# A two-layer hybrid trunk on one core: joint feed-forward weights loaded after the first down product, gate matmuls written later, the second mixer at half pace, and q, k, v loaded a chunk ahead

## The chip, the cores and the metric

The kernel runs on one core of one Trainium2 chip. The metric is the device time in microseconds of one execution. TensorE (PE in the profile) does the matmuls and the 128x128 transposes, VectorE (DVE) and ScalarE (ACT) the elementwise work, GpSimd (POOL) a few subtractions and powers, and SyncE (SP) issues every load and store.

## The reference

The input is x of 1024 rows and 1024 columns in float32. Two layers follow, each with a mixer and a SwiGLU feed-forward between RMS norms:

```python
h = _rmsnorm(x, pre_mix_g[layer])
h = mixer(h)                                   # layer 0: conformer conv + RG-LRU; layer 1: mLSTM
x = x + _rmsnorm(h, post_mix_g[layer])
h = _swiglu(_rmsnorm(x, pre_ffn_g[layer]), ...)  # (silu(x Wg) * (x Wu)) Wd, 2816 hidden columns
x = x + _rmsnorm(h, post_ffn_g[layer])
```

The mixer of layer 0 multiplies the normed rows with one input projection of 2048 columns. One half goes through a gated causal convolution of 31 taps, a LayerNorm and a swish (the conformer). The other half goes through a convolution of 4 taps, two sigmoid gates from a block-diagonal matmul, a linear recurrence and a product with a GeLU branch (the LRU). The concatenated results go through an output projection. The mixer of layer 1 is an mLSTM: q, k, v, an output gate and two gate rows per head come from one projection, and a matrix memory of 8 heads is carried along the rows in chunks.

## The kernel before, in words

All wide products are done as three matmuls of float32 halves: each operand is split into a rounded part (hi, a cast on ACT) and a remainder (lo, a subtraction on DVE or POOL), and `mm3` (L124 to L128) adds hi·hi, hi·lo and lo·hi in PSUM. The 1024 rows are worked in two halves of 512 rows, A and B, so that the mixer or norm of one half stands beside the matmuls of the other.

**Written order and order on the engines.** The main line of matmuls is a set of Python generators. `run` (L1165) steps one of them, and each of its steps has a cost. `step` (L1145) adds cost times pace to every side generator that was handed to `start` (L1140), and advances it once per whole unit. So the pace says how densely a side's instructions are written between the main line's. When the program is built, a scheduler takes, for each engine, the earliest written instruction whose inputs and buffers are ready by its own reckoning. The written order is thus a priority and not the order in which an engine runs. On the chip each engine, and SP as well, works through its list in order and waits at its head.

**Buffers.** The pools set how far work can run ahead: 5 `raw` weight tiles of 512 KB (`raw_tile`, L87), 4 `hi` and 4 `lo` tiles (L90), 30 `unit` and 13 `small` tiles (L51), 4 PSUM banks for the main line and 4 (`ps_aux`) for everything else.

**Layer 0.** `in0` (L711) computes the 16 blocks of the input projection. `mixer0` (L863) alternates between `lrus` (L848) and `conformer` (L803). The conformer's 31 taps are 30 operations on DVE per tile (`pcv`, L754), four tiles to a half. `lru` (L767) runs the 4-tap convolution into `xr` and then, for each of two gates, takes a PSUM tile `pg`, yields once, and writes the matmul (L775), which reads `xr`. Mixer A runs at pace 1.2 beside `in0` of both halves. After 12 of the 16 blocks of half B come the output projection of half A (`Project`, `popA`/`pooA` tiles) with `sandwich` (L202, post-norm, residual, pre-norm and the transposes `ptnoA`) as a side, the last 4 blocks of half B with their GeLU (`gel`, L729), and then `phase0` of the feed-forward for 10 of its 11 blocks. Mixer B starts before the last chunk of that projection, at the pace `PACE_B` of 1.2. It has to be done before the output projection of half B (`pooB`), which follows `phase0(EARLY)`.

**Feed-forward.** Both halves together go through a Strassen-like scheme with 11 blocks of hidden columns. `phase0` computes the products of half A. `down_first` (L594) is the first of the down products: for each of 11 blocks `prep2` (L558) loads one raw tile `r20a` (layer 1: `r21a`), splits it into `whid0a` and `wlod0a`, and 12 matmuls add into the tiles `d`. Beside it `feature_b` transposes half B (`ptnoB`, `ptnpB`) and makes the sums and differences of the two halves (`xs`, `xb`, `xa`, `xk`) with DVE. `phase1` needs these and the joint weights: `prep1a` (L432) loads four raw tiles for a block (`ri`, `rj` of gate and up) and two products of phase 0 (`u2`), forms eight differences on POOL (`t14`, `t23`) and splits `rj`; `prep1b` (L460) splits the differences. `f.begun = f.prep1a(0)` is written before `down_first`, in both layers.

**Layer 1.** `in1` writes v (24 steps), then 8 blocks of q and k, then 8 blocks of the output gate o (`pimo`). For half B the first 32 steps stand beside `mlstm` of half A, which then is drained; the 8 blocks of o follow the output projection of half A (`popA`), beside `sandwich`. `mlstm` (L949) works in 4 chunks of 128 rows per half: at the head of a chunk SP loads the broadcast decay rows `ab` (written a moment before to `da`) and `iwb`, then `qk` and `vt`; PE transposes k (`pk`, L1011), multiplies q and k (`sc`), the scores with v (`pn`), updates the state (`pu`), and transposes the result (`ph`, L1090) after a norm on ACT, POOL and DVE.

Of the kernel before, what the change touches and what calls it, by code (L numbers as in the profile page):

```python
# [14 lines left out]
P = 128  # L15
# [25 lines left out]
def trunk(ctx: ExitStack, tc: tile.TileContext, x, w_in, w_out, w_gate, w_up, w_down,  # L41
# [12 lines left out]
    def unit(shape, dt=F32, name="u"):  # L54
        return up.tile(shape, dt, tag="u", name=name, bufs=NU)
# [269 lines left out]
    class Ffn:  # L325
# [146 lines left out]
        def phase1(self, ms):  # L472
            l = self.l
            ms = list(ms)
            w_next = self.prep1b(ms[0], *self.begun)
            for _ in self.rest:
                pass
            for n, m in enumerate(ms):
                w, h11 = w_next
                u2 = [w[k]["u2"] for k in range(2)]  # L480
                u3, c21, b, c = [], [], [], []
                for k in range(2):
                    a = ps_main(f"pa{l}{m}{k}")
                    self.product(a, w[k]["t2"], self.ops["s2"], True)
                    TT(u2[k], a, u2[k], op=OP.add)
                    yield 2.8
                for k in range(2):
                    b.append(ps_main(f"pb{l}{m}{k}"))
                    self.product(b[k], w[k]["t3"], self.ops["s3"], True)
                    u3.append(small([P, T], f"u3{l}{m}{k}"))  # L490
                    TT(u3[k], b[k], u2[k], op=OP.add)
                    yield 2.8
                if n + 1 < len(ms):
                    w_next = self.prep1(ms[n + 1])
                for k in range(2):
                    c.append(ps_aux([P, T], f"pc{l}{m}{k}"))
                    self.product(c[k], w[k]["t1"], self.ops["s1"], True)
                    TT(u3[k], c[k], u3[k], op=OP.add)
                    yield 2.8
                nc.scalar.activation(u3[0], u3[0], AF.Silu)  # L500
                for k in range(2):
                    self.product(b[k], w[k]["t4"], self.ops["a22"], False)
                    c21.append(small([P, T], f"c21{l}{m}{k}"))
                    TT(c21[k], b[k], u2[k], op=OP.add)
                    yield 2.8
                TT(u3[0], u3[0], u3[1], op=OP.mult)
                nc.sync.dma_start(self.d_s["a22"][m], u3[0])
                nc.scalar.activation(c21[0], c21[0], AF.Silu)
                for k in range(2):
                    self.product(c[k], w[k]["b22"], self.ops["s4"], False)  # L510
                    TT(u2[k], c[k], u2[k], op=OP.add)
                    yield 2.8
                nc.scalar.activation(u2[0], u2[0], AF.Silu)
                TT(c21[0], c21[0], c21[1], op=OP.mult)
                TT(u2[0], u2[0], u2[1], op=OP.mult)
                self.sums(m, h11, u2[0], c21[0], u3[0])
# [250 lines left out]
    def lru(m, j, res):  # L767
# [4 lines left out]
        for i in range(2):  # L772
            ps = ps_aux([P, T], f"pg{h}{j}{i}")
            yield
            nc.tensor.matmul(ps, lw[:, i * 4 + j], xr, start=True, stop=True)  # L775
            s = small([P, T], f"sg{h}{j}{i}")
            nc.scalar.activation(s, ps, AF.Sigmoid, bias=V(("b_a", "b_x")[i], j))
            g.append(s)
# [170 lines left out]
    def mlstm(m):  # L949
# [39 lines left out]
        nc.sync.dma_start(d_w[h], iw)  # L989
        yield  # L990
        m.yT = []
        for c in range(NT):
            cs = slice(c * P, (c + 1) * P)
            ab = unit([P, 8, P], F32, f"ab{h}{c}")
# [2 lines left out]
            dw = d_w[h].rearrange("(a s) j -> s a j", s=2)  # L997
            for s in range(2):
                nc.sync.dma_start(iwb[s * 64:(s + 1) * 64], dw[s, :, cs].partition_broadcast(64))
            qk = unit([P, 8, P], F32, f"qk{h}{c}")  # L1000
            nc.sync.dma_start(qk, d_qk[h][:, :, cs].rearrange("a p j -> p a j"))
            vt = unit([P, 8, 129], F32, f"vt{h}{c}")
            nc.sync.dma_start(vt, d_v[h][c])
            pc = ps_aux([P, 40], f"pc{h}{c}")
            nc.tensor.transpose(pc, ce[:, cs], ident[0:40, 0:40])
            cem = sp.tile([P, 40], F32, tag="cem", name=f"cem{h}{c}", bufs=2)
# [49 lines left out]
            if not (h == 1 and c == NT - 1):  # L1056
                for i in range(4):
# [3 lines left out]
                    for s in range(2):  # L1061
# [2 lines left out]
                                                       iwb[rr, i, P - 1:P], pu[rr, s],  # L1064
                                                       op0=OP.mult, op1=OP.add)
                    yield
            ss = sp.tile([P, 8], F32, tag="hss", name=f"hss{h}{c}", bufs=2)
            for hd in range(8):
                junk = sp.tile([P, P], BF16, tag="junkh", name=f"jh{h}{c}{hd}", bufs=1)
# [53 lines left out]
    W.pool = len(W.src)  # L1123
    src_in1()
    src_in1()
    o_part = W.src[-8:]
    del W.src[-8:]
    src_proj(m_out, OUT1)
    W.src += o_part
    src_ffn(1, EARLY)  # L1130
# [9 lines left out]
    def start(gen, pace):  # L1140
        s = [gen, pace, 0.0]
        sides.append(s)
        return s
# [50 lines left out]
    run(gb, CUT)  # L1194
    until(sa, lambda: all(4 + j in ma.yT for j in range(4)))
    oa = Out("oA")
    ga = start(sandwich(oa, x, x1, post_mix[0:1], 0, gf(0), f0.feature_a), 1.2)
    sb = []

    def second_mixer():  # L1200
        drain(sa)
        sb.append(start(mixer0(mb), PACE_B))

    run(Project(ma.yT, oa, OUT0).run(second_mixer))
    sb = sb[0]
    run(gb)
    drain(ga)
    run(f0.phase0(EARLY))
    drain(sb)
    ob = Out("oB")  # L1210
    gb = start(sandwich(ob, x, x1, post_mix[0:1], 1, gf(0), f0.feature_b, 6), 1.0)
    run(Project(mb.yT, ob, OUT0).run())
    run(f0.phase0(LATE))
    f0.begun = f0.prep1a(0)
    run(f0.down_first())
    drain(gb)
    run(f0.phase1(range(HP)))
# [9 lines left out]
    gb = in1(nb, xmb)  # L1227
    run(gb, 32)
    drain(sa)
    pa = Out("pA")  # L1230
    ga = start(sandwich(pa, x2, x3, post_mix[1:2], 0, gf(1), f1.feature_a), 1.2)
    run(Project(na.yT, pa, OUT1).run())
# [6 lines left out]
    gb = start(sandwich(pb, x2, x3, post_mix[1:2], 1, gf(1), f1.feature_b, 6), 1.0)  # L1239
    run(Project(nb.yT, pb, OUT1).run())  # L1240
    run(f1.phase0(LATE))
    f1.begun = f1.prep1a(0)
    run(f1.down_first())
    drain(gb)
    run(f1.phase1(range(HP)))
# [95 lines left out]
```

## Time and profile before

| | us |
|---|---|
| median of 3 runs | 2179.38 (2175.66 to 2179.52) |
| the profiled execution | 2178.53 |
| its span, first to last instruction | 2176.7 |
| PE busy | 2071.7 (95%) |
| DVE busy | 1476.4 (68%) |
| ACT busy | 919.6 (42%) |
| POOL busy | 680.2 (31%) |

The profiled execution is 1.8 us longer than its span. A PE instruction's end is modelled and neighbours overlap, so busy time on PE is time in which it had something in hand, at whichever clock was granted: the granted clock of a stretch is given as a share of full speed, 1.00 for 2.4 GHz and 0.50 for 1.2 GHz.

### The profile page before, as it was taken

Reading aid. Unit: us, or ns where it says so; the run is one execution under the profiler, and the core shown is the slowest. Engines: PE = TensorE matmul, PEld = TensorE weight load, DVE = VectorE, ACT = ScalarE, POOL = GpSimd, SP = SyncE. Lnnn points to the kernel's source line nnn. Section 1 sums busy time; section 2 is a strip of 40 time slices with the busy share of each in tenths; the row PEclk is TensorE's granted clock in tenths of the full one; section 3 lists DMA queues with packets and bytes.
Section 4 is the critical chain, followed back from the end, with each engine's and each line's share of the span. In section 5 each row is a group of like instructions: output and inputs, shape, how many; then the busy total and the mean of one; then the engine's idle time right before and its main releaser. Section 6 shows DMA issues by size and latency. Waiting matters only on the chain.

```text
span 2176.7 us, 26097 instructions
## 1 busy us (share of the span) xinstructions
PE 2071.7 (95%) x9200; PEld 1680.8 (77%) x9200; DVE 1476.4 (68%) x2037; ACT 919.6 (42%) x1304; POOL 680.2 (31%) x453
## 2 busy tenths in 40 slices
PE   7989979997999999999999998999998999999998
PEld 6767756775888887787988987778876788888786
DVE  7999859347666677558653754546458977766567
ACT  5665575545222222446253333545445222223453
POOL 4344533443533436501010000300024544436311
PEclk9999989997999999999999999999999999999999
DMA  6232434555444459967473752657456544469966
GB/s 229 74 126 89 135 142 163 169 179 185 168 160 165 165 174 319 395 206 250 133 251 104 224 191 84 233 184 220 147 187 213 188 150 162 159 218 350 335 220 225
DMA packets 202739, 417.38 MB, mean 192 GB/s; under 512 B 19920, under 2 KB 48720, under 8 KB 202608
## 3 DMA queue, kind: packets, MB, share of 16 engines
q1 hardware_dynamic: 202608, 415.72, 56.0%
q8 instruction: 72, 1.18, 0.2%
q14 instruction: 59, 0.48, 0.1%
HBM read 302.82 MB, written 112.82 MB: 191 GB/s over the span
## 4 chain that ended last, share of the span: by engine, by line
PE 72%; DVE 13%; DMA 6%; issue 5%; ACT 3%; POOL 1%; SPq 0%; DVEq 0%; POOLq 0%; ACTq 0%
PE d L127 5%; PE d L128 5%; PE d L126 5%; DVE pcv L754 4%; PE pb L127 4%; PE pb L126 3%; PE pb L128 3%; PE pc L128 3%; PE pc L127 3%; PE pc L126 3%; PE p L126 3%; PE p L127 3%; PE p L128 3%; PE pa L128 2%; PE pa L126 2%
## 5 line engine op out<-in xcount | busy, mean ns | idle before, releaser
L107 ACT CAST whi<-raw 128x1024 fp32r<-128x1024 f32 (+2 forms) x164 | 164.3, 1005 | 234.1 <-PE pimo L127 49.9
L109 POOL TENSOR_TENSOR wlo<-raw,whi 128x1024 fp32r<-128x1024 f32 x66 | 166.6, 2530 | 230.6 <-ACT whi L107 192.4
L109 DVE TENSOR_TENSOR wlo<-raw,whi 128x1024 fp32r<-128x1024 f32 (+2 forms) x98 | 112.0, 1146 | 132.8 <-ACT whi L107 127.1
L754 DVE SCALAR_TENSOR_TENSOR pcv<-cy,vec,pcv 128x512 f32<-128x512 f32 x240 | 166.7, 746 | 0.6
L1078 POOL TENSOR_TENSOR hrr<-hss,half 128x8 f32<-128x8 f32 x8 | 13.1, 1641 | 251.5 <-DVE hss L1076 251.5
L132 DVE TENSOR_TENSOR wlod1s<-r21s,whid1s 128x1024 fp32r<-128x1024 f32 x44 | 55.2, 1260 | 49.1 <-ACT whid1s L131 48.6
L132 DVE TENSOR_TENSOR wlod0s<-r20s,whid0s 128x1024 fp32r<-128x1024 f32 x44 | 59.9, 1362 | 41.1 <-ACT whid0s L131 37.9
L126 PE MATMUL p<-xTnoA,whi 128*128 128x512 f32 x176 | 71.5, 411 | 7.7 <-ACT gel L729 5.9
L131 ACT CAST whid1s<-r21s 128x1024 fp32r<-128x1024 f32 x44 | 46.3, 1053 | 65.9 <-PE d L128 50.9
L131 ACT CAST whid0s<-r20s 128x1024 fp32r<-128x1024 f32 x44 | 46.3, 1053 | 61.1 <-PE d L128 54.1
L128 PE MATMUL p<-xTnoA,wlo 128*128 128x512 f32 x176 | 72.1, 413 | 0.0
L127 PE MATMUL p<-xTnoA,whi 128*128 128x512 f32 x176 | 71.5, 406 | 0.0
L127 PE MATMUL d<-wlod0s,whid0s 128*128 128x512 f32 x176 | 69.5, 395 | 2.1 <-DVE wlod0s L132 2.0
L126 PE MATMUL p<-xTnpA,whi 128*128 128x512 f32 x176 | 70.8, 405 | 0.0
L128 PE MATMUL p<-xTnpA,wlo 128*128 128x512 f32 x176 | 70.6, 401 | 0.0
L127 PE MATMUL p<-xTnpA,whi 128*128 128x512 f32 x176 | 70.2, 399 | 0.0
L127 PE MATMUL d<-wlod1s,whid1s 128*128 128x512 f32 x176 | 69.7, 396 | 0.0
L128 PE MATMUL d<-whid1s,wlod1s 128*128 128x512 f32 x176 | 69.5, 395 | 0.0
L128 PE MATMUL d<-whid0s,wlod0s 128*128 128x512 f32 x176 | 68.7, 390 | 0.0
L132 DVE TENSOR_TENSOR wlod0a<-r20a,whid0a 128x1024 fp32r<-128x1024 f32 x33 | 44.3, 1348 | 34.7 <-ACT whid0a L131 33.2
L126 PE MATMUL d<-whid1s 128*128 128x512 f32 x176 | 63.7, 397 | 3.2 <-ACT yeA L624 3.2
L548 POOL TENSOR_TENSOR wt<-wq 128x512 f32<-128x512 f32 x22 | 35.4, 1610 | 89.6 <-DMA wq<-in_w_down 44.0
(2483 smaller groups left out, 6660.7 us busy)
## 6 DMA issues: line engine op xcount, KB each, us to landing
wq<-in_w_down SPq DMA_DIRECT2D x88, 256.0 KB, 5.1
ft<-wt SPq DMA_DIRECT2D x88, 256.0 KB, 5.1
raw<-in_w_in SPq DMA_DIRECT2D x32, 512.0 KB, 3.5
raw<-in_m_in SPq DMA_DIRECT2D x32, 512.0 KB, 4.5
raw<-in_w_gate SPq DMA_DIRECT2D x22, 512.0 KB, 4.3
raw<-in_w_up SPq DMA_DIRECT2D x22, 512.0 KB, 3.8
fp<-p1f SPq DMA_DIRECT2D x44, 256.0 KB, 2.5
fs<-s SPq DMA_DIRECT2D x44, 256.0 KB, 2.3
```

Source lines behind the costliest of these rows:

```text
L107: nc.scalar.copy(hi[:, 0:n], raw[:, 0:n])
L109: eng.tensor_tensor(lo[:, 0:n], raw[:, 0:n], hi[:, 0:n].bitcast(F32), op=OP.subtract)
L126: nc.tensor.matmul(ps, l[0], r[0], start=first, stop=False, **kw)
L127: nc.tensor.matmul(ps, l[0], r[1], start=False, stop=False, **kw)
L128: nc.tensor.matmul(ps, l[1], r[0], start=False, stop=last, **kw)
L131: nc.scalar.copy(dst_hi, src)
L132: nc.vector.tensor_tensor(dst_lo, src, dst_hi.bitcast(F32), op=OP.subtract)
L548: sub(t[0][:, 0], q[0][:, 1], q[0][:, 0], op=OP.subtract)
L754: nc.vector.scalar_tensor_tensor(dst, src[:, k:k + T], V(wname, w0 + k), dst, op0=OP.mult, op1=OP.add)
L1078: nc.gpsimd.tensor_tensor(rr, ss, half, op=OP.pow)
```

## The change

Six edits. (1) In both layers `prep1a(0)` no longer stands before `down_first`; `phase1` calls the whole `prep1` for its first block, after `down_first` and after the side with `feature_b` is drained. (2) In `lru`, the first of the two gate matmuls is written four yields later. (3) Mixer B starts at pace 0.5 and goes to 1.2 when `phase0(EARLY)` begins. (4) `sandwich` of half A in layer 0 waits four steps before its transposes. (5) In `mlstm`, `qk` and `vt` of a chunk are loaded one chunk earlier: those of the first chunk before its `ab`, those of the next after the state update of this one. (6) In layer 1 two of the eight blocks of o of half B are written after `mlstm` of half A is drained, ahead of the output projection of half A; the list of weights is reordered to match.

```diff
         def phase1(self, ms):
             l = self.l
             ms = list(ms)
-            w_next = self.prep1b(ms[0], *self.begun)
+            w_next = self.prep1(ms[0])
...
             ps = ps_aux([P, T], f"pg{h}{j}{i}")
             yield
+            if i == 0:
+                for _ in range(4):
+                    yield
             nc.tensor.matmul(ps, lw[:, i * 4 + j], xr, start=True, stop=True)
...
+        def load(c):
+            qk = unit([P, 8, P], F32, f"qk{h}{c}")
+            nc.sync.dma_start(qk, d_qk[h][:, :, c * P:(c + 1) * P].rearrange("a p j -> p a j"))
+            vt = unit([P, 8, 129], F32, f"vt{h}{c}")
+            nc.sync.dma_start(vt, d_v[h][c])
+            return qk, vt
+
+        loaded = load(0)
         for c in range(NT):
...
-            qk = unit([P, 8, P], F32, f"qk{h}{c}")
-            nc.sync.dma_start(qk, d_qk[h][:, :, cs].rearrange("a p j -> p a j"))
-            vt = unit([P, 8, 129], F32, f"vt{h}{c}")
-            nc.sync.dma_start(vt, d_v[h][c])
+            qk, vt = loaded
...
+            if c + 1 < NT:
+                loaded = load(c + 1)
             ss = sp.tile([P, 8], F32, tag="hss", name=f"hss{h}{c}", bufs=2)
...
-    o_part = W.src[-8:]
-    del W.src[-8:]
+    o_part = W.src[-6:]
+    del W.src[-6:]
...
-    ga = start(sandwich(oa, x, x1, post_mix[0:1], 0, gf(0), f0.feature_a), 1.2)
+    ga = start(sandwich(oa, x, x1, post_mix[0:1], 0, gf(0), f0.feature_a, 4), 1.2)
...
-        sb.append(start(mixer0(mb), PACE_B))
+        sb.append(start(mixer0(mb), 0.5))
...
     drain(ga)
+    sb[1] = PACE_B
     run(f0.phase0(EARLY))
...
-    f0.begun = f0.prep1a(0)
     run(f0.down_first())
...
     drain(sa)
+    run(gb, 2)
     pa = Out("pA")
...
-    f1.begun = f1.prep1a(0)
     run(f1.down_first())
```

## Rows read from the trace of the kernel before

**Rows 1.** The page's first part: busy time, share of the span, instructions.
```profile
PE 2071.7 (95%) x9200; PEld 1680.8 (77%) x9200; DVE 1476.4 (68%) x2037; ACT 919.6 (42%) x1304; POOL 680.2 (31%) x453
```

**Rows 2.** PE's waits over the span: us in total, times, longest us.
```profile
PE d L126 <- ACT whid0a L131: 16.0, 6, 4.3
PE pg L775 <- DVE xr L754: 11.3, 2, 6.3
...
PE ptnoA L349 <- ACT xnnoA L167: 8.6, 3, 5.0
...
PE ph L1090 <- DVE nu L1080: 6.0, 1, 6.0
PE p L126 <- ACT gel L729: 5.9, 2, 3.0
PE pk L1011 <- DMA qk<-dqk: 3.8, 2, 2.0
```

**Rows 3.** Stretches: length, busy (x) of PE, PEld, DVE, ACT, POOL; PEclk, DMA, GB/s.
```profile
123.90:136.40 12.50, 6.23 (x13) 4.22 (x14) 12.50 (x19) 4.59 (x5) 5.67 (x2) 0.59 0.29 101
55.00:247.00 192.00, 183.35 (x758) 143.00 (x757) 189.89 (x264) 115.10 (x142) 74.66 (x35) 0.97 0.28 94
...
283.00:307.10 24.10, 17.76 (x63) 13.04 (x63) 8.41 (x11) 15.31 (x20) 10.76 (x9) 0.78 0.35 131
302.00:419.00 117.00, 110.23 (x445) 85.22 (x446) 91.65 (x109) 74.98 (x99) 43.82 (x18) 0.96 0.44 147
338.90:348.00 9.10, 4.16 (x6) 2.00 (x7) 9.10 (x12) 2.27 (x3) 2.34 (x1) 0.63 0.69 230
481.00:543.00 62.00, 44.59 (x160) 33.43 (x159) 44.30 (x54) 33.32 (x50) 20.76 (x13) 0.81 0.60 201
1205.60:1215.00 9.40, 7.38 (x32) 6.99 (x33) 8.34 (x26) 2.51 (x3) 0.00 (x0) 0.64 1.07 279
1312.40:1324.20 11.80, 5.58 (x17) 4.44 (x18) 8.24 (x23) 3.28 (x10) 1.64 (x1) 0.71 0.13 46
...
1614.80:1669.50 54.70, 44.97 (x189) 34.52 (x188) 42.02 (x46) 29.97 (x41) 22.66 (x14) 0.91 0.71 245
```

**Rows 4.** Timeline of SP's issues, 480 to 531 us: start, us, instruction.
```profile
482.02 0.33 SPq L561 DMA_DIRECT2D r20a<-fa  x1
...
490.55 0.32 SPq L561 DMA_DIRECT2D r20a<-fa  x1
...
521.35 0.33 SPq L442 DMA_DIRECT2D ri01g<-in_w_gate  x1
...
529.55 0.33 SPq L443 DMA_DIRECT2D rj01u<-in_w_up  x1
```

**Rows 5.** Timeline of DVE, 481 to 520 us.
```profile
489.26 1.26 DVE L132 TENSOR_TENSOR wlod0a<-r20a,whid0a 128x1024 fp32r<-128x1024 f32 x1 [2.91 <-ACT whid0a L131]
492.91 1.77 DVE L382 TENSOR_TENSOR xsnoB<-xbnoB,xknoB 128x512 f32<-128x512 f32 x1 [2.39 <-ACT xknoB L379]
...
507.84 0.68 DVE L382 TENSOR_TENSOR xsnoB<-xbnoB,xknoB 128x512 f32<-128x512 f32 x1
```

**Rows 6.** Timeline of POOL, 486 to 500 us: first and last of eight differences.
```profile
486.95 1.26 POOL L448 TENSOR_TENSOR t1400g<-rj00g,ri00g 128x512 f32<-128x512 f32 x1
...
497.59 1.60 POOL L451 TENSOR_TENSOR t1400u<-ri00u,t2300u 128x512 f32<-128x512 f32 x1
```

**Rows 7.** Timeline of DVE, 392 to 403 us: the end of mixer B.
```profile
399.74 2.50 DVE L843 TENSOR_TENSOR acc<-acc,lnq 128x512 f32<-128x512 f32 x4
```

**Rows 8.** The page's costliest groups: the conformer's taps; busy us, mean ns of one.
```profile
L754 DVE SCALAR_TENSOR_TENSOR pcv<-cy,vec,pcv 128x512 f32<-128x512 f32 x240 | 166.7, 746 | 0.6
```

**Rows 9.** Timeline of DVE, 1392 to 1403 us: the last transposed tiles of half A.
```profile
1399.70 2.71 DVE L353 SCALAR_TENSOR_TENSOR xTnpA<-ptnpA,vec,xTnpA 128x512 fp32r<-128x512 f32 x4
```

**Rows 10.** Timeline of PE, 1417 to 1418 us: phase 0 of layer 1 begins.
```profile
1417.63 0.39 PE L126 MATMUL p<-xTnpA,whi 128*128 128x512 f32 x1
1417.86 0.39 PE L127 MATMUL p<-xTnpA,whi 128*128 128x512 f32 x1
```

## The prediction

> **What bounds the kernel now.** I read the page's first part first: PE is busy for 2071.7 us of a span of 2176.7 [rows 1], so 105 us are idle on PE and everything else runs beside it. The second view is the list of PE's waits [rows 2]. The reader should see that a few names hold most of those 105 us, and that nearly each is the target of one edit: `d` on its split weights, `pg` on `xr`, `ptnoA` on `xnnoA`, `ph` on `nu`, `p` on `gel`, `pk` on the load of `qk`. The third view is busy time by stretch around each wait [rows 3]. There the granted clock counts too: after each of the longer gaps it stands below 1.00, so PE repeats its loss at half speed. I reckon a stretch's price as its idle time (length less PE busy) plus (1 − clock) × PE busy. That is an estimate, since some of the slow time lies inside the gap. The same rows give DVE's idle time, which caps what an earlier PE can use. The fourth view is the timeline of SP, DVE and POOL at the dearest place [rows 4 to 6].
>
> The sum is made against the profiled execution, 2178.5 us (span 2176.7 and 1.8 around it); the median of the runs shown is 2179.4, 0.04% away. About 0.2% (4.4 us) is what a measurement can tell from no change.
>
> **Joint weights, layer 0 (edit 1).** Each `r20a` load is issued 0.03 us after the `wlod0a` of the load before ends: 489.26 + 1.26 = 490.52 and 490.55 [rows 4, 5], and the one before at 482.02 likewise. So one raw tile is going round. The other four hold `ri` and `rj` of block 0 until their differences and their split are done, and PE waits through load, cast and subtraction for every 12 matmuls. The edit moves behind these loads on SP's list four raw loads, two `u2` loads and, on POOL, eight differences, from 486.95 to 499.19 [rows 6]. Then five raw tiles go round, and the `fx` loads for `feature_b`, which stand in the same SP queue, wait less too. In 481 to 543 PE idles 62.00 − 44.59 = 17.4 us and loses 0.19 × 44.59 = 8.5 to the clock: 25.9 at most. DVE idles 62.00 − 44.30 = 17.7 in the same stretch [rows 3], and `phase1` needs DVE's sums of the halves before its first product. So 17.7 is the nearer cap, and since the eight differences now fall where DVE is full I take **15**.
>
> The first differences of `phase1` must not come late. Their four raw tiles come free with the splits of blocks 6 to 9 of `down_first`, as those of block 1 do now: issued from 521.35 to 529.55 [rows 4], 21 to 13 us ahead of the stretch's end at 543. POOL needs three of its eight differences, three eighths of 12.2 us or 4.6, before the first cast. That cover is enough. If it were gone, each layer would pay 8.2 (the four issues), 12.2 (POOL) and 2.4 for a cast and a subtraction, each taken at the 1.2 of `wlod0a` [rows 5], 22.8 in all. So the term lies between −22.8 and 25.9.
>
> How much POOL costs DVE: the same subtraction takes 0.68 us at 507.84 and 1.77 at 492.91, beside POOL [rows 5]. Four such cost some 4 us, which the 15 includes. The Trainium skill (SBUF — State Buffer, Who interferes with whom) says that a DVE instruction with two SBUF inputs and a GpSimd instruction that reads SBUF exclude one another for the whole instruction. This speaks against the edit; by it DVE would lose up to all of POOL's 12.2 us and the term would be some 7. The trace agrees that they collide, at 1.09 us each.
>
> **Joint weights, layer 1.** In 1614.8 to 1669.5 PE idles 9.7 and loses 0.09 × 44.97 = 4.0; DVE idles 12.7 [rows 3]. Half B is normed later there, so part of DVE's idle time comes before the work that it could do. I take **7**, between −22.8 and 13.8.
>
> **Gate matmuls (edit 2).** `pg` waits for `xr` twice, 6.3 and 5.0 us [rows 2]. Mixer A: 6.3 idle and 0.41 × 6.23 = 2.6 of clock [rows 3]. But from 55 to 247 DVE idles 2.1 us of 192 [rows 3]: it is the bound there, and a PE that passes the gate waits later for the LayerNorm's sums. So **2**, between 0 and 8.9. Mixer B stands beside `phase0`, whose matmuls don't need the mixer: 4.9 idle and 0.37 × 4.16 = 1.5 of clock in 338.9 to 348.0. Four yields let PE do `p` first; I take **5** of 6.5.
>
> **Mixer B at half pace (edit 3).** The last chunk (8 steps of 2.6) and four blocks of 5.2 cost 41.6: at 1.2 that is 50 steps of mixer B written before `phase0`, at 0.5 it is 21. ACT then meets fewer gates ahead of `gel`, whose lateness costs PE 5.9 [rows 2]. With the clock, 283.0 to 307.1 loses 6.3 + 0.22 × 17.76 = 10.2 [rows 3]. The scheduler fills an idle DVE with any ready work whatever the pace, so I take **4**. What is late next is mixer B: it ends at 402 [rows 7], and its output projection begins where the stretch to 419 ends. Half of the 29 steps are the conformer's, of three taps at 166.7 / 240 = 0.69 us [rows 8]: 30 us; the lru's half I put at 10. That is 40 against 25.4 us of idle DVE in 302 to 419 [rows 3]. If all were pushed behind, PE would wait 15 us at `pooB` and lose some 3 to the clock, as after the gate; so the term goes from −18 to 10.2.
>
> **Four more steps for the first sandwich (edit 4).** `ptnoA` waits 8.6 us in all [rows 2]. The transposes wait for row tiles that come from DVE, ACT and loads at their own rate; when they are written later, PE does the same blocks first and then waits for the last row tile as before. **0**, between −3 (one wait's average is 2.9) and 8.6.
>
> **q, k, v a chunk ahead (edit 5).** `pk` waits twice, 3.8 us [rows 2]; the first costs 2.0 and 0.36 × 7.38 = 2.7 of clock [rows 3]: 6.4 in all. Loaded ahead of `ab`, `qk` is there. But SP now has two loads before `ab`, on which DVE and the scores wait, and two more `unit` tiles of 30 are held. I take **5**, between −3.8 (the same waits, moved to `ab`) and 6.4.
>
> **Two o blocks earlier (edit 6).** The last `ph` waits 6.0 for the norm of its chunk. With the clock, 1312.4 to 1324.2 loses 6.2 + 0.29 × 5.58 = 7.8 [rows 3]. The two blocks are ready and fill this. What is late next is the sandwich of half A, with 6 instead of 8 blocks beside it: two blocks are 2 × 24 matmuls at 0.23 us from start to start [rows 10], 11 us, and the transposed tiles end at 1402.4 [rows 9] with `p` at 1417.6 [rows 10], so 15 us of cover stand against 11. **6**, between 0 and 7.8.
>
> **Sum.** 15 + 7 + 2 + 5 + 4 + 0 + 5 + 6 = 44, so 2178.5 − 44 = 2134.5; I say **2135**.
>
> **The rivals.**
> - *VectorE takes the place of each wait.* In the stretches of edits 1 and 2 DVE is nearly full once its waits for casts go, and the differences on POOL slow it. Then layer 0 gives 6, layer 1 gives 2, mixer B's gate 2, and edits 5 and 6 four each: 18, so 2160. For it: 189.9 of 192 busy [rows 3]. Against: 30 us of idle DVE in the two `down_first` stretches. The Trainium skill's rule on who interferes with whom (SBUF — State Buffer) points to this rival.
> - *The edits of written order change little.* The scheduler places what is ready, and edits 2 to 4 leave the engines' lists as they were; the rest gives 33: 2145.5. For it: pace sets a priority alone.
> - *Mixer B comes late to `pooB`.* 18 us back: 2153. Against: only the second chunk needs the conformer, 96 matmuls at 0.23 us [rows 10] or 22 us after the first.
> - *Slower: joint weights late at `phase1`.* If `r20a` keeps all five raw tiles to the end, the four loads, POOL's differences and the split start only then: 22.8, and 2.6 of clock as after the gate of mixer A, per layer; 51 for two against the 44 gained: 2186. It decides from 22 us of PE idle per layer at the first `pa`. Against: block 1's loads get their tiles 13 us or more ahead now [rows 4].
>
> **How the numbers follow.** My forecast (2118 to 2148) gets 0.50, more than it (toward 2115, where DVE's caps and the clock prices are all earned) 0.03, VectorE 0.15, no effect of the order 0.12, late mixer 0.08, slower 0.08, and gains and new waits that cancel 0.04. The range 2112 to 2170 holds the first rivals and leaves about 0.15 out. Faster 0.86, within 0.2% 0.05, slower 0.09.
>
> **What would show it.** Right: `r20a` issues in bursts of five; no wait of `d` over 2 us; clock 1.00 in both stretches; `pg`, `gel` and `pk` gone from PE's waits; `pimo` between `pu` and the last `ph`. Wrong: `pa` waiting for `whit2` or `xs2` at the head of `phase1`; `pm` waiting as long in mixer A as `pg` did (then edit 2 gave nothing there); `pooB` waiting for `ysoB`; `ab` waiting for its load longer than before. A chain of waits with a larger share of DVE would speak for the first rival.

## The result and the profile after

The changed kernel takes 2152.77 us (median of 4 runs, 2149.44 to 2155.18) beside 2178.78 for the kernel before (4 runs, 2175.66 to 2179.52): a ratio of 0.9882, 95% interval 0.9865 to 0.9899. That is 26 us faster, where 44 were predicted. The profiled execution took 2149.44 us, the shortest of its four, with a span of 2147.7: 29.0 less than before.

The page's first part of the changed kernel stands against [rows 1]:

```profile
PE 2055.8 (96%) x9200; PEld 1670.3 (78%) x9200; DVE 1481.8 (69%) x2037; ACT 923.9 (43%) x1308; POOL 679.5 (32%) x453
```

PE's waits over the span, changed kernel, against [rows 2] (us in total, times, longest):

```profile
PE pa L126 <- ACT whit210g L131: 9.3, 1, 9.3
PE d L127 <- DVE wlod0a L132: 6.7, 6, 2.8
PE ptnoA L349 <- ACT xnnoA L167: 5.9, 2, 4.2
PE pa L128 <- DVE wlot200u L132: 4.8, 1, 4.8
PE pa L126 <- ACT whit200g L131: 4.4, 1, 4.4
PE pa L126 <- ACT whit210u L131: 3.5, 1, 3.5
...
PE d L126 <- ACT yfA L624: 3.1, 1, 3.1
PE pg L778 <- ACT acc L764: 2.8, 1, 2.8
PE pn L1060 <- DVE pr L1050: 2.7, 2, 1.7
...
PE pg L778 <- DVE xr L754: 1.8, 1, 1.8
...
PE pg L778 <- DVE xTnoA L353: 0.7, 1, 0.7
```

Nearly every wait of [rows 2] is gone or cut: `d` on `whid0a` (16.0), `pg` (11.3, now 5.3 in three waits of other sizes), `ph` (6.0, now 1.0), `gel` (5.9, now 0.5), `pk`. The wait of `d` for `wlod0a` is not: 2.6 of its 6.7 us still fall into `down_first` of layer 0. New names stand in the list: `pa` on `whit2` and `wlot2`, which is the head of `phase1`, and `d` on `yfA`, which is phase 2 of layer 0.

Where the time came from is read from the start of the same PE instruction in both traces. Each line is the point up to which the shift has been earned:

| point | before | changed | shift | this stage alone | predicted |
|---|---|---|---|---|---|
| last `pooB` | 468.8 | 456.8 | -12.0 | -12.0 (edits 2 to 4) | -11 |
| last `d` of `down_first`, layer 0 | 542.3 | 504.8 | -37.5 | -25.5 (edit 1) | |
| first `pa` of block 2 | 595.8 | 575.9 | -19.9 | +17.6 (edit 1) | -15 for both |
| last `d` of phase 2, layer 0 | 1045.2 | 1027.9 | -17.2 | +2.7 | 0 |
| last `pimq` | 1304.8 | 1286.3 | -18.5 | -1.3 (edit 5) | -5 |
| first `p` of layer 1 | 1417.6 | 1393.0 | -24.6 | -6.1 (edit 6) | -6 |
| last `d` of `down_first`, layer 1 | 1669.1 | 1629.1 | -40.1 | -15.6 (edit 1) | |
| first `pa` of block 2 | 1730.9 | 1702.4 | -28.5 | +11.6 (edit 1) | -7 for both |
| last `d` of the kernel | 2168.6 | 2139.1 | -29.5 | -1.0 | 0 |

Each column is one execution. The same program was executed a second time (the first kernel under "Is it the joint weights that are late?"): its stages agree with the changed column within 1.4 us, but the stage up to the last `d` of phase 2 of layer 0 took 4.5 us more. The +2.7 of that line is smaller than this spread.

Edit 1 won in `down_first` almost all that PE lost there, and then gave back two thirds in layer 0 and three quarters in layer 1 at the head of `phase1`. Busy time in these four stretches of the changed kernel (the columns of [rows 3]):

```profile
469.10:504.80 35.70, 33.12 (x156) 26.83 (x155) 31.09 (x37) 22.64 (x30) 10.80 (x8) 1.00 0.74 254
504.80:575.90 71.10, 58.86 (x231) 46.00 (x230) 55.85 (x60) 25.37 (x38) 39.32 (x25) 0.90 0.51 176
1590.20:1629.10 38.90, 38.90 (x189) 32.15 (x187) 32.58 (x34) 22.07 (x29) 14.85 (x11) 1.00 0.81 277
1629.10:1702.40 73.30, 60.54 (x242) 47.75 (x241) 71.24 (x72) 31.18 (x47) 46.29 (x27) 0.88 0.54 182
```

`down_first` now runs with the clock at 1.00 and PE full or nearly so. The head of layer 0 (504.8 to 575.9) has 12.2 us of idle PE and loses 0.10 × 58.86 = 5.9 to the clock, 18.1 together; the same stretch took 53.5 us before, with PE never idle, and takes 17.6 more now. What PE waits for there is seen on ACT and DVE, timelines of the changed kernel:

```profile
506.47 0.62 ACT L131 CAST xs2noB<-xanoB 128x512 fp32r<-128x512 f32 x1 [1.52 <-DVE xanoB L384]
...
508.47 1.06 ACT L131 CAST whit200g<-t2300g 128x1024 fp32r<-128x1024 f32 x1
...
514.62 2.18 ACT L131 CAST xs4noB<-xknoB 128x512 fp32r<-128x512 f32 x4
516.70 1.04 ACT L131 CAST whit200u<-t2300u 128x1024 fp32r<-128x1024 f32 x1
```

```profile
504.79 1.65 DVE L384 TENSOR_TENSOR xanoB<-xsnoB,xanoB 128x512 f32<-128x512 f32 x1
506.47 1.64 DVE L388 TENSOR_TENSOR xknoB<-xknoB,xanoB 128x512 f32<-128x512 f32 x1
508.04 1.75 DVE L132 TENSOR_TENSOR xs2noB<-xanoB,xs2noB 128x512 fp32r<-128x512 f32 x1
...
519.16 5.14 DVE L132 TENSOR_TENSOR xs4noB<-xknoB,xs4noB 128x512 fp32r<-128x512 f32 x4
524.23 2.28 DVE L132 TENSOR_TENSOR wlot200u<-t2300u,whit200u 128x1024 fp32r<-128x1024 f32 x1
```

And on POOL, the last difference that each kind's first split needs:

```profile
497.30 2.27 POOL L449 TENSOR_TENSOR t2300g<-rj00g,t1400g 128x512 f32<-128x512 f32 x1
...
507.53 1.71 POOL L449 TENSOR_TENSOR t2300u<-rj00u,t1400u 128x512 f32<-128x512 f32 x1
```

`t2300g` is ready at 499.57, but its cast comes at 508.47: it stands on ACT behind `xs2noB`, which waits for DVE's `xanoB`. `t2300u` is ready at 509.24, its cast comes at 516.70 and its subtraction at 524.23, behind the casts and subtractions of `feature_c` (`xs1`, `xa22`, `xs4`). DVE has no gap from 504.8 to 532.7 us, and beside POOL's differences its 128x512 operations take 1.64 to 1.77 us instead of the 0.68 of [rows 5]. So the theory after the first look was: DVE is full at the head of `phase1`, stretched by POOL. The rival was the prediction's own fourth: the joint weights' loads and differences come late.

### The profile page after: what moved, and what is told of

Its sections match the earlier page's. It is cut to its first block, busy times and chain, and to the rows that moved or that the text cites. A ratio compares the mean times of both kernels' runs of the same rounds, so it can differ in the third digit from the quotient of the medians.

```text
span 2147.7 us, 26103 instructions
## 1 busy us (share of the span) xinstructions
PE 2055.8 (96%) x9200; PEld 1670.3 (78%) x9200; DVE 1481.8 (69%) x2037; ACT 923.9 (43%) x1308; POOL 679.5 (32%) x453
## 4 chain that ended last, share of the span: by engine, by line
PE 64%; DVE 16%; DMA 7%; issue 6%; ACT 4%; POOL 2%; SPq 0%; DVEq 0%; POOLq 0%; ACTq 0%
DVE pcv L754 5%; PE d L127 4%; PE d L128 4%; PE d L126 4%; PE pb L128 4%; PE pb L126 4%; PE pb L127 4%; PE pc L128 3%; PE pc L127 3%; PE pc L126 3%; PE p L126 3%; PE p L127 3%; PE p L128 3%; PE pa L128 2%; PE pa L127 2%
## 5 line engine op out<-in xcount | busy, mean ns | idle before, releaser
L132 DVE TENSOR_TENSOR wlod1s<-r21s,whid1s 128x1024 fp32r<-128x1024 f32 x44 | 60.6, 1383 | 43.7 <-ACT whid1s L131 41.2
L132 DVE TENSOR_TENSOR wlod0a<-r20a,whid0a 128x1024 fp32r<-128x1024 f32 x33 | 46.1, 1403 | 25.8 <-ACT whid0a L131 23.6
L498 DVE TENSOR_TENSOR u<-pc,u 128x512 f32<-128x512 f32 x44 | 30.2, 689 | 46.1 <-PE pc L128 46.1
```

The source lines that it names most:

```text
L132: nc.vector.tensor_tensor(dst_lo, src, dst_hi.bitcast(F32), op=OP.subtract)
```

## The experiments

All ratios are against the kernel before on the same chip.

**The edits apart.** Four kernels, each the kernel before with a part of the change: edit 1; edits 2 to 4; edit 5; edit 6 (their lines in the diff above).

> The kernel before with edit 1 alone (joint weights behind the first down product). Theory (the work on block 0's joint weights and DVE's full list at the head of phase 1 give back most of what the down product gains): the d products end some 25 us earlier in layer 0 and 15 in layer 1, PE then waits 12 us or more per layer for whit2 and wlot2, and the whole is 12 us faster than before (8 and 4). Rival (the give-back in the changed kernel comes from the other edits, which bring PE there too early for DVE): the waits at phase 1 stay under 4 us per layer and the whole is 22 us faster, as forecast.

> The kernel before with edits 2, 3 and 4 alone (gate matmuls later, second mixer at half pace, sandwich waits four steps). Theory (their gain is PE time in layer 0 up to pooB and is kept to the end): pooB begins 13 us earlier, and the whole is 13 us faster. Rival (a later stage is bound by a chain that does not start earlier, so the gain is eaten there): pooB begins 13 us earlier and the whole is under 5 us faster.

> The kernel before with edit 5 alone (q, k, v a chunk ahead). Theory (the wait of pk goes, and waits of pn for pr take its place because ab is what the scores wait for): 1 to 2 us faster, within what can be told from no change; PE's list has pn waiting 1 to 2 us at the first chunks instead of pk. Rival (my term): 5 us faster, no such waits.

> The kernel before with edit 6 alone (two o blocks ahead of the output projection of half A). Theory (the blocks fill the wait of the last ph): 6 us faster, ph waits about 1 us, and phase 0 of layer 1 starts 6 us earlier. Rival (the sandwich, with two blocks less beside it, gives it back): 0 to 2 us faster, with p or ptnpA waiting ahead of phase 0.

| kernel | median us (runs) | ratio, 95% interval |
|---|---|---|
| before | 2174.42 (24) | |
| edit 1 | 2162.1 (5) | 0.9946, 0.9934 to 0.9959 |
| edits 2 to 4 | 2173.74 (11) | 0.9998, 0.9988 to 1.0008 |
| edit 5 | 2174.47 (11) | 1.0006, 0.9997 to 1.0015 |
| edit 6 | 2168.47 (8) | 0.9972, 0.9958 to 0.9986 |

Edits 1 and 6 gave what the theories said. The four parts add up to 0.0078 (17 us), where the whole change gave 0.0118 (26 us). Edit 5 gave nothing: PE's waits of the first mixer of layer 1, in the run of edit 5 alone, show that another releaser stood behind the load (before: `pk` on the load of `qk`, 2.0, in the same stretch).

```profile
PE ph L1098 <- DVE nu L1088: 6.0, 1, 6.0
PE pn L1057 <- DVE pr L1047: 1.5, 2, 1.0
```

Edits 2 to 4 were the surprise. They arrive at the first `pooB` 12.1 us early, still 9.9 early at the end of `phase1`, and only 2.0 early at the end of phase 2 of layer 0. The theory that they are kept to the end fell: by these two profiles most of the gain is eaten in phase 2. PE's waits in that stretch (840 to 1044 us), run of edits 2 to 4:

```profile
PE d L127 <- DVE wlod0a L132: 3.9, 4, 2.6
PE d L126 <- DVE yfA L619: 3.8, 1, 3.8
```

Before, that second wait was 0.6.

**Is it the joint weights that are late?** Two changes to the changed kernel, alone and together, and a third kernel without edits 2 to 4. First, `feature_c` written behind the first two pairs of products:

```diff
             w_next = self.prep1(ms[0])
-            for _ in self.rest:
-                pass
...
                     TT(u3[k], b[k], u2[k], op=OP.add)
                     yield 2.8
+                if n == 0:
+                    for _ in self.rest:
+                        pass
```

Second, block 0 loaded ahead of `down_first` again, into `unit` tiles, so that five raw tiles go round:

```diff
-                ri = raw_tile([P, D], f"ri{name}")
+                ri = (unit if own else lambda s, name: raw_tile(s, name))([P, D], name=f"ri{name}")
...
+    f0.begun = f0.prep1a(0, True)
     run(f0.down_first())
```

> The changed kernel with one thing moved: the sums of feature_c (xs1, xa22, xs4 and their splits), which phase 1 writes ahead of its first product, stand behind its first two pairs of products. Theory (VectorE and ScalarE are full there, and feature_c's casts and subtractions stand ahead of the second kind's split): the waits of pa for the up kind, 3.5 and 4.8 us in layer 1, 1.2 and more in layer 0, go, and the kernel is 5 to 12 us faster than the changed one, so 2141 to 2148 where that has 2153. Rival (the joint weights' loads and GpSimd's differences come late): the wait of pa for the gate kind, 4.4 and 9.3 us, is untouched and the up kind waits for its differences instead; within 3 us of 2153. A second rival: the sums are late at pc instead, and the wait moves there; within 3 us as well.

> The changed kernel, but with block 0's joint weights loaded ahead of down_first again, as before the change, in four unit tiles of their own, so that down_first still has five raw tiles. Theory that VectorE is full at the head of phase 1: the differences on GpSimd move back beside feature_b in down_first and slow VectorE there, d gives back a few us, pa waits less; the two about cancel, within 6 us of 2153. Rival that the late joint weights cost the time at the head of phase 1 (17.7 us in layer 0, 11.6 in layer 1 given back after d): the waits of pa for whit2 and wlot2 go and most of that comes back, 15 to 25 us faster, 2128 to 2138.

> Both of the two: own unit tiles for block 0's joint weights, loaded ahead of down_first, and feature_c behind the first two pairs of products. If VectorE's queue is the cause, what it gains over own_tiles is what the moved sums gained alone, 5 to 12 us; if the loads are, it equals own_tiles. If it is the sum of both, about 2125 to 2140, the best of all versions.

> The changed kernel without the gate matmuls' delay, the half pace and the sandwich's four steps (edits 2 to 4 undone; 1, 5 and 6 stay). Theory, from the run of 2 to 4 alone: their 10 us at the output projection of half B are eaten in phase 2 of layer 0 in any company, so this equals the changed kernel within 3 us (2150 to 2156). Rival: beside edit 1 they are kept, since down_first and phase 1 then follow at another rhythm; this is 6 to 10 us slower than the changed kernel, 2159 to 2163.

| kernel | median us (runs) | ratio, 95% interval |
|---|---|---|
| before | 2175.85 (9) | |
| `feature_c` written later | 2153.9 (4) | 0.9898, 0.9883 to 0.9913 |
| own tiles | 2162.26 (5) | 0.9942, 0.9930 to 0.9955 |
| both | 2163.23 (5) | 0.9940, 0.9928 to 0.9953 |
| without edits 2 to 4 | 2156.61 (4) | 0.9915, 0.9901 to 0.9928 |

The first and the third row test nothing. The lists of all engines came out the same as without the moved lines, over the whole kernel: the first is the changed kernel run again, the third is own tiles run again. Moving the written line did not move one instruction, so `feature_c` stands ahead of the up kind's split as before, and that own tiles and "both" took the same time says nothing on loads or sums. What the pairs do show is how far one program repeats. The ratios lie 0.0016 and 0.0002 apart, and phase 2 of layer 0 of the changed program took 198.6 us in one profile and 203.1 in the other:

```profile
829.30:1027.90 198.60, 188.56 (x824) 151.91 (x823) 125.51 (x126) 87.99 (x99) 53.60 (x40) 0.99 0.80 281
```

```profile
828.60:1031.70 203.10, 190.42 (x824) 152.59 (x823) 125.36 (x126) 87.91 (x99) 57.11 (x40) 0.98 0.79 276
```

The row "`feature_c` written later" is thus the changed kernel, measured beside the other rows of this table, and they are compared with it here.

Own tiles missed both expectations: a ratio 0.0044 above that of the changed kernel beside it, some 8 us slower. In layer 0 `whit200g` ended 1.2 us ahead of `d`'s last matmul instead of 4.7 behind it, and `wlot200u` 8.0 behind instead of 21.7. So the weights were there 6 and 14 us earlier, and still the stretch to block 2 took 74.1 us instead of 71.1. PE waited for something else, PE's waits over the span:

```profile
PE pa L126 <- ACT y L601: 39.8, 2, 23.2
```

`y` is the copy that frees `d`'s PSUM tiles. On ACT it stood behind `feature_b`'s casts, which waited for DVE's `xan` (7.0 us in layer 0, 12.7 in layer 1), because `feature_b` itself was late: its last `xs2noB` is cast at 521.85, 19 us after `d`, where that is 506.47, 1.7 after `d`, in the changed kernel. SP's timeline in layer 1 shows one cause, the loads of half B queued behind a joint weight that waited for its raw tile.

```profile
1625.40 0.33 SPq L442 DMA_DIRECT2D ri12g<-in_w_gate  x1
...
1626.73 0.42 SPq L374 DMA_DIRECT2D xknpB<-fx  x1
```

So this kernel trades late weights for a late `feature_b`; against the rival it shows only that early weights alone buy nothing while the sums come late.

Without edits 2 to 4 the kernel takes 2156.61 us, 2.7 more than the changed kernel beside it, and the two intervals overlap. That fits the theory (within 3 us) better than the rival (6 to 10): beside edit 1, too, little of these edits reaches the end. Its last `pooB` starts at 467.1 us, 9.6 later than in the profile of the changed kernel beside it, but its phase 2 of layer 0 takes 196.0 us against 203.1.

**What eats the gain in phase 2, and what stretches the head.** The length of phase 2 of layer 0 (last `pc` to last `d`) sorts the profiles so far, one of each kernel: 194.6 to 197.6 us in the five kernels without edits 2 to 4 together (195.1 before), 198.6 to 203.1 in the five with them. The gap between the groups, 1.0, is smaller than what one program repeats to, but no profile lies on the wrong side. The instruction lists differ there: in the second five DVE has a 13th `wlod0s`, of the next product, ahead of the four sums into `yfA` that free the PSUM tiles for it; SP's loads stand in another order too. I take it that the scheduler came to that choice by its reckoning of the times before it; no run shows its steps. Three kernels, each the changed one with a single edit: mixer B at pace 0.6, which happens to give back both lists; block 0's differences on DVE; and `feature_c` without the splits of `xa22` and `xs4`.

```diff
-        sb.append(start(mixer0(mb), 0.5))
+        sb.append(start(mixer0(mb), 0.6))
```

```diff
-            sub = nc.gpsimd.tensor_tensor
+            sub = (nc.vector if m == 0 else nc.gpsimd).tensor_tensor
```

```diff
-            for n, key in enumerate(("s1", "a22", "s4")):
-                for k, fs in enumerate(later):
-                    cast(key, k, fs[n])
-                yield
+            for k, fs in enumerate(later):
+                cast("s1", k, fs[0])
+            yield
+            for key in ("a22", "s4"):
+                self.ops[key] = self.ops["s1"]
+            yield
```

> The changed kernel with one number changed: mixer B starts at pace 0.6 instead of 0.5. In the five profiles that have edits 2 to 4 together the stretch from the last first-use of pc to the end of phase 2's products of layer 0 takes 198.6 to 203.1 us, in the five without them 194.6 to 197.6; in the five the list of VectorE has one more split (wlod0s) ahead of the four sums into yfA that free the PSUM tiles of the next product, and SP's loads stand in another order. With pace 0.6 both lists of phase 2 are word for word those of the kernel before. Theory (the loss is that order, which the builder's scheduler arrived at): the stretch takes 195 to 197.5, the wait of d for yfA falls under 1 us, mixer B's gain at pooB stays, and the kernel is 3 to 7 us faster than the changed one, a ratio of about 0.985. Rival (an earlier arrival at phase 2 meets the loads at a worse time, whatever the order): the stretch stays at 199 to 203 and the ratio at 0.988 to 0.990.

> The changed kernel with the eight differences of block 0 (t14, t23), in both layers, on VectorE instead of GpSimd. Theory (VectorE is full at the head of phase 1, and GpSimd's differences stretch its operations from 0.69 to 1.65-1.79 us): VectorE takes on 8 times 0.69, 5.5 us, and is spared about 1.0 us on each of the 9 operations that ran beside the differences in layer 0; the stretch from d's last matmul to the first of block 2 shortens by 2 to 6 us a layer, so the kernel is 2 to 10 us faster than the changed one. Rival (what pa waits for is the differences themselves, which come late behind their loads): on VectorE, behind the other work, they come no sooner and the stretch is as long or longer; 2153 to 2160.

> The changed kernel without the splits of xa22 and xs4: 8 casts and 8 subtractions a layer less, and the products that use them take the split of xs1 instead. Only the head of phase 1 is read here. Theory (these subtractions, 7.6 us of a full VectorE with GpSimd beside it, and the casts stand ahead of the up kind's split): wlot200u ends 6 to 8 us earlier against d's last matmul than its 21.7 us, the wait of pa for the up kind goes, and the stretch from d's last matmul to block 2's first pa falls from 71.1 us by 5 to 8. Rival (the up kind's differences on GpSimd, ready 4.4 us after d, or its loads): wlot200u still ends 20 us or more after d's last matmul.

| kernel | median us (runs) | ratio, 95% interval |
|---|---|---|
| before | 2175.41 (9) | |
| mixer B at 0.6 | 2142.89 (5) | 0.9849, 0.9834 to 0.9863 |
| block 0's differences on DVE | 2138.95 (4) | 0.9837, 0.9822 to 0.9852 |
| without two of `feature_c`'s splits | 2134.96 (1) | |

The last kernel does less work than the others, so its time is no gain; only the head of `phase1` is read.

Pace 0.6 did as the theory said: phase 2 takes 194.8 us, and `d` waits 0.7 for `yfA`. DVE's timeline where the sums stand, first of the run of edits 2 to 4, then of pace 0.6:

```profile
910.49 1.97 DVE L132 TENSOR_TENSOR wlod0s<-r20s,whid0s 128x1024 fp32r<-128x1024 f32 x1 [1.49 <-ACT whid0s L131]
912.37 2.47 DVE L619 TENSOR_TENSOR yfA<-d,v 128x512 f32<-128x512 f32 x4
```

```profile
892.58 2.47 DVE L619 TENSOR_TENSOR yfA<-d,v 128x512 f32<-128x512 f32 x4
894.98 1.21 DVE L132 TENSOR_TENSOR wlod0s<-r20s,whid0s 128x1024 fp32r<-128x1024 f32 x1
```

In the first the sums stand behind a split that had itself waited 1.49 us; in the second the split follows them. Over all profiles of this document the order sorts without exception, apart from the kernel without two splits, whose list is a third one (193.7 us): with the split ahead, six profiles of four programs, phase 2 takes 198.6 to 203.1 us, 201.8 on the mean, and `d` waits 3.1 to 4.1 for `yfA`; with the sums ahead, seven, it takes 194.5 to 197.6, 195.3 on the mean, and `d` waits 0.2 to 1.3. The rival of an early arrival does not fit, since pace 0.6 arrives earlier than the changed kernel. But the wait makes up only 2.7 of the 6.5 us. In five of the six the clock is 0.94 over the 30 us from the first sum, where the seven have 1.00, which is 1.7 more; the rest is not assigned, and no run changed DVE's list without SP's.

Not all of pace 0.6's gain is there: against the changed kernel's profile 3.6 us were won ahead of phase 2 (2.7 of them by the last `pooB`) and 3.8 in it. By the end of the two profiles only 1.8 are left, since the profiled execution of pace 0.6 was the slowest of its five (2147.61); by the medians it is 0.0033 to 0.0049 faster than the two series of the changed kernel. Against the kernel without edits 2 to 4 (0.9915) it is 0.0066 faster, 14 us: with the sums ahead, what these edits win by `pooB` reaches the end.

Differences on DVE did what the theory said, in layer 0 slightly more than its 2 to 6 us: the stretch to block 2 fell from 71.1 to 64.2 us and from 73.3 to 67.5, and `down_first` of layer 0 was 3.1 us shorter. Busy time in the same four stretches:

```profile
468.90:501.50 32.60, 32.60 (x156) 26.95 (x156) 28.02 (x38) 22.63 (x30) 2.67 (x3) 1.00 0.79 280
501.50:565.70 64.20, 56.65 (x230) 44.06 (x229) 56.48 (x66) 25.06 (x38) 41.08 (x21) 0.95 0.56 193
1583.60:1622.50 38.90, 38.90 (x189) 32.10 (x186) 31.76 (x43) 25.15 (x35) 2.98 (x4) 1.00 0.83 279
1622.50:1690.00 67.50, 61.25 (x243) 47.73 (x242) 66.98 (x71) 28.12 (x42) 50.84 (x25) 0.90 0.54 188
```

DVE took on 8 operations in each layer and was busy less: 28.02 + 56.48 = 84.5 us in the two stretches of layer 0, against 31.09 + 55.85 = 86.9. Its timeline shows why:

```profile
500.35 0.69 DVE L384 TENSOR_TENSOR xanoB<-xsnoB,xanoB 128x512 f32<-128x512 f32 x1
501.07 0.69 DVE L388 TENSOR_TENSOR xknoB<-xknoB,xanoB 128x512 f32<-128x512 f32 x1
501.68 0.68 DVE L448 TENSOR_TENSOR t1400g<-rj00g,ri00g 128x512 f32<-128x512 f32 x1
...
514.86 2.49 DVE L132 TENSOR_TENSOR xs4noB<-xknoB,xs4noB 128x512 fp32r<-128x512 f32 x4
```

The differences now come later against `d`'s last matmul (`t2300g` ready 2.7 us after it, where it was 5.3 ahead; `t2300u` 5.7 after it, where it was 4.4), and `pa` still starts sooner (3.9 us after it, where it was 4.8). That is the plainest evidence against late weights.

It also sizes the collision. From the last `pooB` to block 2 the kernel before takes 127.0 us, the changed kernel 119.1 and this one 109.0; from the first `p` of layer 1 to its block 2 the three take 313.3, 309.4 and 304.4. So edit 1 is worth 7.9 and 3.9 us with the differences on POOL, and 18.0 and 8.9 with them on DVE, more than the 15 and 7 of the prediction. Of what comes back at the head, 10.7 and 5.7 us remain with the differences on DVE; that these are the work of `feature_b` and `feature_c` behind `d` is read from the timelines and was not tested apart.

What the collision is, the two engines' starts show. In the changed kernel, from 504 to 510 us, DVE and POOL take turns: DVE starts an operation every 1.6 to 1.7 us (504.79, 506.47, 508.04), and so does POOL:

```profile
504.17 1.72 POOL L450 TENSOR_TENSOR t2300u<-rj00u 128x512 f32<-128x512 f32 x1
505.85 1.71 POOL L451 TENSOR_TENSOR t1400g<-ri00g,t2300g 128x512 f32<-128x512 f32 x1
```

Alone, DVE starts one every 0.60 us (as 501.07 and 501.68 above) and POOL one every 1.25 (own tiles, layer 1):

```profile
1627.75 1.29 POOL L450 TENSOR_TENSOR t2310g<-rj10g 128x512 f32<-128x512 f32 x1
1629.00 1.29 POOL L449 TENSOR_TENSOR t2310g<-rj10g,t1410g 128x512 f32<-128x512 f32 x1
```

A pair thus takes nearly as long as one after the other, 1.85; side by side it would take 1.25. And where DVE has its work ready without a gap, POOL does not get its turn at all: in the run with the differences on DVE, POOL's first difference of block 1 stood beside eleven of DVE's splits that followed one another at 0.60 us each, and ended 1.2 us after DVE went on to `u200g`, which reads one of its two inputs from PSUM.

```profile
510.61 7.89 POOL L448 TENSOR_TENSOR t1401g<-rj01g,ri01g 128x512 f32<-128x512 f32 x1 [35.01 <-DMA rj01g<-in_w_gate]
```

Leaving out two of `feature_c`'s splits, `wlot200u` ended 12.5 us after `d`'s last matmul, 9.2 earlier, and the waits of `pa` for the up kind went, as the theory said. The stretch to block 2 fell by only 1.9, not by 5 to 8: it was 9.1 us ahead at the first `pa` of block 1 and lost 7.2 again before block 2, where `pb` waited 3.1 us for DVE's `u` and the clock then stood at 0.50 for 6.8 us. In layer 1 it fell by 4.1, from 73.3 to 69.2. So the up kind's split was not what set the length of the head.

**Both gains together.** With the differences on DVE and pace 0.5, DVE's list has the split ahead of the sums again (phase 2 takes 200.7 us); by the expectation below so it does at pace 0.6, which was not run. At 0.7 the sums are ahead.

```diff
-            sub = nc.gpsimd.tensor_tensor
+            sub = (nc.vector if m == 0 else nc.gpsimd).tensor_tensor
...
-        sb.append(start(mixer0(mb), 0.5))
+        sb.append(start(mixer0(mb), 0.7))
```

> The changed kernel with block 0's differences on VectorE and mixer B at pace 0.7; with these two the lists of phase 2 of layer 0 stand as in the kernel before (with pace 0.6 and the differences on VectorE they don't). Theory: the two gains add, since they lie in different stretches: 0.0045 from the differences and 0.0033 from the order of phase 2, a ratio of about 0.980 (2131 to 2136 beside 2175 of before), with phase 2 of layer 0 at 195 to 197.5 us and the wait for yfA under 1 us. Rival (phase 2's length has nothing to do with that order, and pace 0.6 was lucky elsewhere): phase 2 stays at 199 to 203 and the ratio at 0.983 to 0.985.

Measured: 2142.21 us (5 runs) beside 2175.78 (9), ratio 0.9846, interval 0.9828 to 0.9865; not better than the differences alone. Phase 2 took 194.5 us and the wait for `yfA` 0.4, as the theory of the order says, and edit 1 was worth 17.5 and 8.1 us here, so both gains are in their stages. But the first `pooB` was only 5.0 us early, where it is 13.2 at pace 0.5 and 14.7 at 0.6. PE's waits from 255 to 420 us in this kernel:

```profile
PE p L126 <- ACT gel L729: 4.8, 2, 4.1
PE p L126 <- ACT sg L422: 3.3, 2, 2.8
PE pg L778 <- DVE xr L754: 2.2, 2, 1.2
```

At 0.5 the wait for `gel` was 0.5. So the denser mixer B brings back the wait that edit 3 removes, and against the run with the differences on DVE 8 us are lost ahead of phase 2. Another way to the sums ahead, at pace 0.5 with the differences on DVE, wasn't tried.

## Why the prediction was right, and where it was off

- **Faster, as forecast, but by 26 instead of 44.** The measured 2153 lies inside the range of 2112 to 2170 and outside the likeliest case's 2118 to 2148. By the ledger of the two profiles 14.5 are missing from 44: 7.1 and 3.0 in edit 1, 3.7 in edit 5, 2.7 up to the end of phase 2 of layer 0, less 1.0 that edits 2 to 4 gave more and 1.1 in the last stages. (The other 3 are that the changed kernel's profile is its fastest execution.) Timed alone, the edits say it otherwise: 12 of 22 from edit 1, nothing of 11 from edits 2 to 4, nothing of 5 from edit 5, 6 of 6 from edit 6.
- **Joint weights, layer 0: the charge "Four such cost some 4 us".** Mis-sized. The cap of 17.7 did not hold for `down_first` itself, where 25.5 of PE's 25.9 were won; but work of `feature_b` and `feature_c` wasn't done when `d` ended, and 17.6 came back at the head of `phase1`. Net 7.9, not 15. With the differences on DVE the net is 18.0, close to the cap. So what POOL's eight differences cost is some 10 us, not 4: they fell on more than four operations, and on a DVE without a gap. That 18.0 meets 17.7 is in part luck, since I had read the cap from one stretch and left out what the next one would have to wait for.
- **"That cover is enough".** Half right. The loads were issued from 487.90 to 498.44, 17 to 6 us ahead of `d`'s end, where I had taken 21 to 13. The gate kind's differences were ready in time, the up kind's 4.4 us after `d`. Neither set the time: with both kinds' differences later still, but on DVE, the head was 6.9 us shorter. The waits of `pa` that I had named as the sign of late weights came, with ACT and DVE behind them.
- **Joint weights, layer 1.** 4.0, not 7, by the same mechanism; `d` gained 15.6, more than the 13.8 at which I had capped the term, and 11.6 came back. With the differences on DVE the net is 8.9.
- **POOL against DVE.** The Trainium skill (SBUF — State Buffer, Who interferes with whom) spoke against the edit. By it I had up to all of POOL's 12.2 us and some 7 for layer 0; measured are 10 and 7.9. The trace agrees with it nearly to the whole instruction: a pair takes 1.6 to 1.7 us, where one after the other would take 1.85 and side by side 1.25. I had read the 1.09 us of one operation as the price and counted four of them.
- **"`r20a` issues in bursts of five".** Wrong: they came one every 2.6 to 3.3 us, at 475.08, 477.65, 480.34 and 483.63. `d` waited 2.6 us all the same in place of 17.3, at most 1.6 at a time, so the sign "no wait over 2 us" came in that stretch.
- **Gate matmuls and half pace.** 11 predicted with edit 4's nothing, 12.0 measured at the last `pooB`, and then lost: alone the edits changed the time by 0.0002, and beside edit 1 by 2.7 us, not clear of noise. Edits 2 to 4 were never run one by one, so the split into 2, 5, 4 and 0 stays open. The step that failed is the one that the sum takes for granted, that what is won before `pooB` is kept: the scheduler's lists change downstream, and phase 2 takes 6.5 us longer on the mean of the profiles with that order of the sums.
- **The rival "mixer B comes late to `pooB`"** did not happen: `pooB` waited 0.9 us, for `sg`. That its time, 2153, is the measured one is chance.
- **q, k, v ahead.** The step "the first costs 2.0 and 0.36 × 7.38" counted the wait as the load's alone. Behind it stood `pr` and `qi` on DVE; 1.3 in the ledger and nothing when timed alone.
- **Two o blocks.** Predicted 6, measured 6.1 in the ledger and 0.0028 alone, 6 us.
- **The first rival, VectorE takes the place of each wait,** had 6 and 2 for edit 1 and was nearer there than the forecast. It failed at edit 6, where it had 4 for 6.1, and at `pooB`, where it had 2 for 12.0; timed alone, though, edits 2 to 4 gave nothing. The measured 2153 lies between it and the likeliest case.
- **The second rival, the edits of written order change little,** is wrong in its reason, since the lists changed and `pooB` came 12 us earlier, and nearly right in the time of edits 2 to 4. Its picture does hold for the moved `feature_c`, which left every list as it was.

## What to carry to other kernels

A gain in one stage is worth what the next stage doesn't have to wait for: add the work that the stage leaves behind, on its fullest engine, to the next one's bill. When VectorE is full, work given to GpSimd beside it can cost VectorE more than doing it there; price both. Where a scheduler builds the lists from a reckoned time, compare the lists before blaming or crediting an edit: here a pace changed by 0.1 reordered a stage that begins some 420 us after that mixer's end, and profiles with the two orders differ by 6.5 us on the mean there, while an edit that moved written lines changed no list at all, in two kernels.

## What the runs showed of the hardware

Eight 128x512 subtractions on GpSimd beside VectorE took 1.5 to 2.3 us each, where one alone takes 1.29 (`t2310g` in the run with own tiles), and VectorE's own went from 0.69 to 1.64 to 1.77; the 128x1024 split went from 1.21 to 2.28. Done on VectorE the same eight take 0.68 each. Where the two engines take turns, a pair starts every 1.6 to 1.7 us, little less than the 0.60 and 1.25 between starts of each alone added up. Where VectorE's operations with two inputs in SBUF follow one another without a gap, they keep their 0.60 us and GpSimd's waits: one took 7.89 us in layer 0 and one 7.18 in layer 1 (the run with the differences on VectorE). The kernel with that exchange alone has a ratio of 0.9837, where the changed kernel has 0.9882 and, the second time, 0.9898.
